# Merged attention heads stored in DRAM as one fp32 word and split where they are loaded, with a fourth probability buffer, in a hybrid encoder block

## The chip, the cores and the metric

The kernel runs on one core of a Trainium2 chip. The metric is the device time of one execution in microseconds (us). Several executions were timed; the profile is of one more execution with the hardware profiler on. MB below means 1024 KB.

## The reference

One layer of an encoder over 1024 tokens plus 16 meta tokens, width 1024, in fp32. Attention and a linear recurrence run side by side from one projection, are merged by gates, projected and followed by a SwiGLU block:

```python
xn = rmsnorm(h, norm1_g[l])
q, k, v, xr, gr, g_merge = jnp.split(xn @ w_in[l], splits, axis=-1)
attn = bidirectional_gqa(rope(q), rope(k), v)      # 8 query heads, 2 kv heads, head size 128
rnn = (rg_lru(xc, ..., False) + rg_lru(xc, ..., True)) * jax.nn.gelu(gr)
mix = g_attn * attn + g_rnn * rnn                  # gates are sigmoids of g_merge
h = h + mix @ w_out[l]
hn = rmsnorm(h, norm2_g[l])
g, u = jnp.split(hn @ w_ffn_in[l], 2, axis=-1)
h = h + (jax.nn.silu(g) * u) @ w_ffn_out[l]
```

The change touches `mix`, on its way from the attention to the product with `w_out`.

## The kernel before, in words

PE multiplies in a form of fp32 that it rounds. So every operand is kept as two halves, a rounded high part and the rest: `split` (line 95) copies the value to the high part on ACT (L96) and subtracts that from the value on DVE or POOL (L97); `mm3` (line 99) makes each product from three matmuls. A head's merged output thus takes twice the space of its fp32 value when it is stored split.

The stage in question is the attention, about 500 to 830 us of the span. It walks over 8 heads `h` and, in each, 8 tiles `i` of 128 queries, so over 64 tiles. `emit_scores` (line 572) does one tile: nine score matmuls into one of two PSUM tiles `S0`, `S1`, row maximum on DVE (L585), exponential on ACT (L588), then the probabilities in two fp16 halves into a buffer `PP` (L594 and L595 on ACT, L597 on DVE) and one transposing DMA (L600) from `PP` to `PT`. There are three `PP` buffers, taken in turn, so a tile writes the one that the transpose of three tiles earlier has read. Every second tile, `emit_pv` (line 604) multiplies the 256 transposed probabilities of two tiles (a *unit* `u`, four in a head) with V in 25 matmuls (L611). That is done two units behind: the product of a unit stands on PE after the scores of the second unit that follows.

Behind the product, `emit_pv` merges: DVE multiplies by the gate (L613), POOL adds the recurrent branch (L614), and the result of 256 columns is split into `mst` (ACT L96, POOL L97) and stored with both halves to `mix_d` in DRAM (L618, on SP's queue). Only the first half of head 7 is split straight into the operand `M` in SBUF (L621).

Between the tiles PE has other work: the gate projection of a later head (`ga_steps`, six matmuls behind a tile, `gap`), and in head 7 the output projection of the first four heads (`out_half`, tile `oph`). For the projection, `load_mix(kh, c)` (line 645) brings four heads of one half of the columns back to SBUF, both halves of the words, with two DMAs issued by POOL (L650) straight into `M`. `load_wout` (line 654) brings a block of `w_out` through one of three `raw` buffers and splits it on ACT and POOL. The table `ahead` (line 694) says behind which tile `(h, i)` these loads are written.

All DMAs but those of `load_mix` stand in one queue, SP's: transposes, loads of Q, of the recurrent branch (`gar`), of weights and of the residual rows (`h`), and the stores. A framework's scheduler orders each engine's instructions; it moves loads ahead of where the program writes them, and a `raw` buffer must be free before SP may issue into it. SP's queue is in order: what waits there holds everything behind it.

Of the kernel before, what the change touches and what calls it, by code (L numbers as in the profile page):

```python
# [8 lines left out]
F32 = mybir.dt.float32  # L9
F32R = mybir.dt.float32r  # L10
F16 = mybir.dt.float16
# [8 lines left out]
T = 1024  # L20
# [3 lines left out]
NH = 8  # L24
# [9 lines left out]
KPAIR = KLO + T  # L34
# [8 lines left out]
def tile_hybrid_encoder_block(  # L43
# [25 lines left out]
    V, S, G, PE, SP = nc.vector, nc.scalar, nc.gpsimd, nc.tensor, nc.sync  # L69

    x = x[0]
    out = out[0]
# [5 lines left out]
    dram = ctx.enter_context(tc.tile_pool(name="dram", bufs=1, space=bass.MemoryType.DRAM))  # L78
# [7 lines left out]
    def page(shape, dtype, name):  # L86
        return pages.tile(shape, dtype, tag="pg", name=name)

    def raw_tile(shape):
        return rawp.tile(shape, F32, tag="raw", name="raw")  # L90

    def f32(ap):
        return ap.bitcast(F32)

    def split(src, hi, lo, eng=None):
        S.activation(out=hi, in_=src, func=AF.Copy)  # L96
        (eng or V).tensor_tensor(out=lo, in0=src, in1=f32(hi), op=ALU.subtract)  # L97

    def mm3(ps, terms):
        n = len(terms)  # L100
        for k, (lh, ll, rh, rl) in enumerate(terms):
            PE.matmul(out=ps, lhsT=lh, rhs=rh, start=(k == 0), stop=False)  # L102
            PE.matmul(out=ps, lhsT=lh, rhs=rl, start=False, stop=False)  # L103
            PE.matmul(out=ps, lhsT=ll, rhs=rh, start=False, stop=(k == n - 1))  # L104
# [10 lines left out]

    q_d = [dram.tile([HD, T], F32, name=f"q_d{h}") for h in range(NH)]
    rm_d = [dram.tile([128, T], F32, name=f"rm_d{b}") for b in range(NB)]
    mix_d = [dram.tile([2, 4, 128, T], F32, name=f"mix_d{kh}") for kh in range(2)]

    def rstd(sq_sum, n, count, tag, scale=1.0):  # L120

# [435 lines left out]
    p2 = p2_pool.__enter__()  # L557
# [3 lines left out]
    def fill_bank(name):  # L561
        return ps2.tile([128, 512], F32, tag="fill", bufs=2, name=name)

    SB = [ps2.tile([128, 3, 512], F32, name=f"S{i}") for i in range(2)]
    PP = [p2.tile([128, KPAIR], F16, bufs=1, name=f"PP{i}") for i in range(3)]
    for p in PP:
        G.memset(p[:, T:KLO], 0.0)

# [3 lines left out]
    def emit_scores(h, i, q):  # L572
        kv = h // 4
        n = n_tile[0]
        n_tile[0] += 1
        s = SB[n % 2]
        pair = PP[n % 3]
        if n < 2:
            PE.matmul(out=s[:, 2, NK - 2 * KC:KC], lhsT=ones, rhs=mask, start=True, stop=True)
        for j in range(3):  # L580
            a, e = KC * j, min(KC * j + KC, NK)
            qs = slice(128 * i, 128 * i + 128)
            mm3(s[:, j, 0:e - a], [(q[:, 0, qs], q[:, 1, qs], kT[:, 0, kv, a:e], kT[:, 1, kv, a:e])])
        nm = small.tile([128, 1], F32, name="nm")
        V.tensor_reduce(out=nm, in_=s[:, :, 0:KC], axis=AX.XY, op=ALU.max, negate=True)  # L585
        p = p2.tile([128, 3, KC], F32, name="p")
        den = small.tile([128, 1], F32, name="den")
        S.activation(out=p, in_=s[:, :, 0:KC], func=AF.Exp, bias=nm, accum_out=den)  # L588
        r = small.tile([128, 1], F32, name="pr")
        V.tensor_scalar(out=den, in0=den, scalar1=2.0 ** -14, scalar2=None, op0=ALU.mult)  # L590
        V.reciprocal(out=r, in_=den)
        pf = p.rearrange("p j k -> p (j k)")[:, 0:NK]

        S.activation(out=pair[:, 0:NK], in_=pf, func=AF.Copy, scale=r)  # L594
        S.activation(out=pair[:, T + 64:T + 64 + NM], in_=pf[:, T:NK], func=AF.Copy, scale=r)  # L595
        for a, e, o in ((0, T, KLO), (T, NK, T + 32)):
            V.scalar_tensor_tensor(out=pair[:, o:o + e - a], in0=pf[:, a:e], scalar=r, in1=pair[:, a:e], op0=ALU.mult, op1=ALU.subtract)  # L597
        if i % 2 == 0:
            PT[h, i // 2] = p2.tile([128, 17, 256], F16, name="PT")
        SP.dma_start_transpose(  # L600
            out=PT[h, i // 2][:, :, 128 * (i % 2):128 * (i % 2) + 128], in_=pair,
        )

    def emit_pv(h, u, gar):
        kv = h // 4
        pt = PT.pop((h, u))
        ps = fill_bank("pv")[:, 0:256]
        vs = slice(HD * kv, HD * kv + HD)
        terms = [(j, 0, j) for j in range(9)] + [(j, 0, 9 + j) for j in range(8)] + [(j, 1, j) for j in range(8)]
        for n, (j, hl, m) in enumerate(terms):  # L610
            PE.matmul(out=ps, lhsT=vt[:, j, hl, vs], rhs=pt[:, m], start=(n == 0), stop=(n == len(terms) - 1))  # L611
        c = slice(256 * u, 256 * u + 256)
        V.tensor_tensor(out=gar[:, 0, c], in0=gar[:, 0, c], in1=ps, op=ALU.mult)  # L613
        G.tensor_tensor(out=gar[:, 1, c], in0=gar[:, 0, c], in1=gar[:, 1, c], op=ALU.add)  # L614
        if h < NH - 1 or u >= 2:
            st = p2.tile([128, 2, 256], F32R, name="mst")
            split(gar[:, 1, c], st[:, 0], st[:, 1], G)
            SP.dma_start(out=mix_d[h // 4][:, h % 4, :, c].rearrange("l d t -> d l t"), in_=f32(st))  # L618
        elif u % 2 == 1:
            cs = slice(256 * u - 256, 256 * u + 256)  # L620
            split(gar[:, 1, cs], M[0][1][0][:, 3], M[1][1][0][:, 3])  # L621

    def load_gar(h):
        g = page([128, 2, T], F32, "gar")
        SP.dma_start(out=g[:, 1], in_=rm_d[h])
        return g
# [15 lines left out]

    M = [[[None, None], [None, None]], [[None, None], [None, None]]]

    def load_mix(kh, c):

        k = 3 if kh and not c else 4
        for hl in range(2):
            M[hl][kh][c] = page([128, 4, 512], F32R, f"M{hl}{kh}{c}")
            G.dma_start(out=M[hl][kh][c][:, 0:k], in_=mix_d[kh][hl, 0:k, :, 512 * c:512 * c + 512].rearrange("h d t -> d h t"))  # L650

    wo = {}

# [31 lines left out]
    def out_steps():  # L685
# [5 lines left out]
    gar = {0: ga0, 1: load_gar(1)}  # L691
    steps = ga_steps(w_ga, gar[1])

    ahead = {
        (6, 4): [(load_mix, 0, 0)],
        (6, 6): [(load_wout, 0, 0), (load_wout, 1, 0)],
        (6, 7): [(load_h, 0, page, [0])],
        (7, 2): [(load_h, 0, page, [1])],
        (7, 3): [(load_wout, 0, 1)],
        (7, 4): [(load_mix, 1, 0)],  # L700
        (7, 5): [(load_wout, 1, 1)],
        (7, 6): [(load_wout, 2, 0)],
        (7, 7): [(load_wout, 3, 0), (load_wout, 2, 1), (load_wout, 3, 1)],
    }
    for h in range(NH):
        for i in range(8):
            emit_scores(h, i, q)
            if i == 1 and h + 1 < NH:
                q_n = load_head(h + 1)
            if i == 3 and h + 2 < NH:  # L710
                w_ga = load_block(COL_GA + 128 * (h + 2), G)
                gar[h + 2] = load_gar(h + 2)
            for fn, *a in ahead.get((h, i), ()):
                fn(*a)
            if i == 5 and h + 2 < NH:
                steps = ga_steps(w_ga, gar[h + 2])
            if (h, i) == (NH - 1, 0):
                steps = out_steps()
            if i % 2 == 1:
                if len(pend) > 1:  # L720
                    u = pend.pop(0)
                    emit_pv(*u, gar[u[0]])
                pend.append((h, i // 2))
            for _ in range(2 if h == 0 and i < 3 else 1):
                next(steps, None)
        q = q_n
    for _ in steps:
        pass
    load_mix(0, 1)
    for k in range(4):  # L730
        if k % 2 == 0 and pend:
            u = pend.pop(0)
            emit_pv(*u, gar[u[0]])
        for _ in out_half(k, 0, 1, SB[k // 3][:, k % 3]):
            pass
# [337 lines left out]
    for n, (i, j) in enumerate(chunks):  # L1073
        if n + AHEAD < len(chunks):
            c = chunks[n + AHEAD]
# [96 lines left out]
```

## Time and profile before

| what | value |
|---|---|
| three timed runs | 1540.11, 1540.17 (median), 1542.09 us |
| the profiled execution | 1543.0 us, of it 1541.2 us from the first to the last instruction |
| PE busy | 1484.2 us, 96% |
| DVE busy | 1101.1 us, 71% |
| ACT busy | 743.1 us, 48% |
| POOL busy | 325.3 us, 21% |
| HBM | 137.15 MB read, 56.36 MB written |

A busy PE is a matmul in flight. Since PE is busy nearly everywhere, the places to look for are the few stretches where it is not, and those where its granted clock is below full speed. The DMA share is the mean busy share of the 16 DMA engines, and goes above 1 where packets of several queues overlap.

### The profile page before, as it was taken

How to read it: one execution, taken by the hardware profiler on the slowest of the kernel's cores; microseconds unless marked ns; L12 is line 12 of the kernel's file. 1: busy time of each engine (PE TensorE's matmuls, PEld its weight loads, DVE VectorE, ACT ScalarE, POOL GpSimd, SP SyncE). 2: the span in 40 equal slices, each digit the busy share in tenths (PEclk: the TensorE clock that was granted, in tenths of full speed). 3: DMA queues.
4: the chain of work that ended last, by engine and by line, in shares of the span. 5: the costliest groups of instructions: out<-in, count | busy, mean ns of one | idle time of the engine just before them, and what ended most of it. 6: DMA issues, size and time to landing. Idle time of an engine off the chain costs nothing. (4 is left out here: it accounts for less than half of the span.)

```text
span 1541.2 us, 20211 instructions
## 1 busy us (share of the span) xinstructions
PE 1484.2 (96%) x7323; PEld 1241.6 (81%) x7323; DVE 1101.1 (71%) x1712; ACT 743.1 (48%) x1264; POOL 325.3 (21%) x243
## 2 busy tenths in 40 slices
PE   6999999999999899997889979999999999999999
PEld 4888888888888788886778857888888888788887
DVE  6888677777776777786764697777777777667562
ACT  5544476677667666666651352322222222364330
POOL 0000000000000544444341253333333333300000
PEclk9999999999999999999999989999999999999999
DMA  6123311122212799999997215444444444699641
GB/s 240 41 77 101 88 33 60 60 62 62 63 55 78 167 201 201 202 199 228 234 228 246 69 40 165 164 157 158 157 157 158 157 158 157 230 378 330 205 149 66
DMA packets 310196, 230.49 MB, mean 150 GB/s; under 512 B 151016, under 2 KB 252352, under 8 KB 310096
## 3 DMA queue, kind: packets, MB, share of 16 engines
q1 hardware_dynamic: 306128, 221.34, 50.9%
q0 software_dynamic: 3968, 7.86, 1.9%
q8 instruction: 57, 0.93, 0.2%
q14 instruction: 43, 0.35, 0.1%
HBM read 137.15 MB, written 56.36 MB: 126 GB/s over the span
## 5 line engine op out<-in xcount | busy, mean ns | idle before, releaser
L96 ACT ACTIVATE wS<-s 128x512 fp32r<-128x512 f32 x88 | 53.2, 628 | 169.2 <-DVE s L880 51.6
L597 DVE SCALAR_TENSOR_TENSOR PP<-p,pr,PP 128x1024 f16<-128x1024 f32 (+1 forms) x128 | 119.4, 986 | 20.2 <-ACT PP L594 20.0
L96 ACT ACTIVATE pw<-pr 128x1024 fp32r<-128x1024 f32 x77 | 81.0, 1061 | 104.8 <-PE po L1088 63.4
L1086 PE MATMUL po<-pw 128*128 128x512 f32 x308 | 120.4, 391 | 1.5 <-ACT pw L96 1.5
L1087 PE MATMUL po<-pw 128*128 128x512 f32 x308 | 120.6, 391 | 0.8 <-DVE pw L97 0.8
L1088 PE MATMUL po<-pw 128*128 128x512 f32 x308 | 120.3, 391 | 0.0
L97 DVE TENSOR_TENSOR pw<-pr,pw 128x1024 fp32r<-128x1024 f32 x77 | 94.0, 1251 | 36.1 <-ACT pw L96 29.7
L611 PE MATMUL pv<-PT,vt 128*128 128x256 f16 x800 | 97.7, 281 | 17.6 <-DMA PT<-PP 16.9
L588 ACT ACTIVATE p<-S,nm 128x1044 f32<-128x1044 f32 x64 | 72.2, 1129 | 68.2 <-DVE nm L585 65.7
L611 PEld LDWEIGHTS <-vt 128*128 128x128 f16 x800 | 78.0, 101 | 33.5 <-issue 18.3
L97 DVE TENSOR_TENSOR wS<-s,wS 128x512 fp32r<-128x512 f32 x88 | 70.5, 818 | 16.9 <-ACT wS L96 16.0
L594 ACT ACTIVATE PP<-p,pr 128x1040 f16<-128x1040 f32 x64 | 73.9, 1155 | 15.2 <-DMA PT<-PP 10.3
L585 DVE TENSOR_REDUCE nm<-S 128x1 f32<-128x1044 f32 x64 | 76.8, 1231 | 2.1 <-PE S L104 2.1
L433 POOL MEMSET xrp<- 128x2 f32 x8 | 0.9, 108 | 349.8 <-DVE xc L440 349.8
L102 PE MATMUL S<-kT,qh 128*128 128x348 f32 (+1 forms) x192 | 63.6, 331 | 6.7 <-ACT p L588 6.4
L1086 PEld LDWEIGHTS po<-pw 128*128 128x128 f32 x308 | 58.1, 189 | 14.1 <-ACT pw L96 1.9
L1087 PEld LDWEIGHTS po<-pw 128*128 128x128 f32 x308 | 58.2, 189 | 13.0 <-DVE pw L97 1.1
L1088 PEld LDWEIGHTS po<-pw 128*128 128x128 f32 x308 | 58.2, 189 | 12.2
L103 PE MATMUL S<-kT,qh 128*128 128x348 f32 (+1 forms) x192 | 62.1, 323 | 0.0
L104 PE MATMUL S<-kT,qh 128*128 128x348 f32 (+1 forms) x192 | 62.0, 323 | 0.0
L97 DVE TENSOR_TENSOR wA<-raw,wA 128x512 fp32r<-128x512 f32 x60 | 50.3, 842 | 15.9 <-ACT wA L96 15.9
L103 PE MATMUL xr<-xn,wblk 128*128 128x264 f32 (+1 forms) x192 | 61.4, 320 | 0.0
(308 smaller groups left out, 4467.0 us busy)
## 6 DMA issues: line engine op xcount, KB each, us to landing
raw<-in_w_ffn_in_dram SPq DMA_DIRECT2D x47, 512.0 KB, 4.8
raw<-in_w_in_dram SPq DMA_DIRECT2D x44, 512.0 KB, 4.1
pr<-act_d SPq DMA_DIRECT2D x77, 256.0 KB, 5.3
raw<-in_w_ffn_out_dram SPq DMA_DIRECT2D x22, 512.0 KB, 4.6
wot_d<-bs SPq DMA_DIRECT2D x44, 256.0 KB, 4.5
act_d<-as SPq DMA_DIRECT2D x44, 256.0 KB, 2.0
pr<-wot_d SPq DMA_DIRECT2D x44, 256.0 KB, 5.3
act_d<-act SPq DMA_DIRECT2D x33, 256.0 KB, 3.3
```

The source lines that it names most:

```text
L96: S.activation(out=hi, in_=src, func=AF.Copy)
L97: (eng or V).tensor_tensor(out=lo, in0=src, in1=f32(hi), op=ALU.subtract)
L102: PE.matmul(out=ps, lhsT=lh, rhs=rh, start=(k == 0), stop=False)
L103: PE.matmul(out=ps, lhsT=lh, rhs=rl, start=False, stop=False)
L585: V.tensor_reduce(out=nm, in_=s[:, :, 0:KC], axis=AX.XY, op=ALU.max, negate=True)
L588: S.activation(out=p, in_=s[:, :, 0:KC], func=AF.Exp, bias=nm, accum_out=den)
L594: S.activation(out=pair[:, 0:NK], in_=pf, func=AF.Copy, scale=r)
L597: V.scalar_tensor_tensor(out=pair[:, o:o + e - a], in0=pf[:, a:e], scalar=r, in1=pair[:, a:e], op0=ALU.mult, op1=ALU.subtract)
L611: PE.matmul(out=ps, lhsT=vt[:, j, hl, vs], rhs=pt[:, m], start=(n == 0), stop=(n == len(terms) - 1))
L1086: PE.matmul(out=banks[t], lhsT=lh, rhs=w[:, 0, 1], start=j == 0, stop=False)
L1087: PE.matmul(out=banks[t], lhsT=lh, rhs=w[:, 1, 1], start=False, stop=False)
L1088: PE.matmul(out=banks[t], lhsT=ll, rhs=w[:, 0, 1], start=False, stop=j == NFP - 1)
```

## The change

It has three parts. The merged head is stored as its fp32 word, 512 columns at a time, from the `gar` tile itself: `mst` and its split are gone. `load_mix` loads the words of two heads at a time through a `raw` buffer, on SP's queue, and splits them there into `M` (ACT and POOL for the first half of the columns, ACT and DVE for the second). A fourth `PP` buffer is added.

```diff
--- before.py
+++ after.py
@@ -115,7 +115,7 @@
 
     q_d = [dram.tile([HD, T], F32, name=f"q_d{h}") for h in range(NH)]
     rm_d = [dram.tile([128, T], F32, name=f"rm_d{b}") for b in range(NB)]
-    mix_d = [dram.tile([2, 4, 128, T], F32, name=f"mix_d{kh}") for kh in range(2)]
+    mix_d = [dram.tile([4, 128, T], F32, name=f"mix_d{kh}") for kh in range(2)]
 
     def rstd(sq_sum, n, count, tag, scale=1.0):
 
@@ -562,7 +562,7 @@
         return ps2.tile([128, 512], F32, tag="fill", bufs=2, name=name)
 
     SB = [ps2.tile([128, 3, 512], F32, name=f"S{i}") for i in range(2)]
-    PP = [p2.tile([128, KPAIR], F16, bufs=1, name=f"PP{i}") for i in range(3)]
+    PP = [p2.tile([128, KPAIR], F16, bufs=1, name=f"PP{i}") for i in range(4)]
     for p in PP:
         G.memset(p[:, T:KLO], 0.0)
 
@@ -574,7 +574,7 @@
         n = n_tile[0]
         n_tile[0] += 1
         s = SB[n % 2]
-        pair = PP[n % 3]
+        pair = PP[n % 4]
         if n < 2:
             PE.matmul(out=s[:, 2, NK - 2 * KC:KC], lhsT=ones, rhs=mask, start=True, stop=True)
         for j in range(3):
@@ -612,12 +612,12 @@
         c = slice(256 * u, 256 * u + 256)
         V.tensor_tensor(out=gar[:, 0, c], in0=gar[:, 0, c], in1=ps, op=ALU.mult)
         G.tensor_tensor(out=gar[:, 1, c], in0=gar[:, 0, c], in1=gar[:, 1, c], op=ALU.add)
-        if h < NH - 1 or u >= 2:
-            st = p2.tile([128, 2, 256], F32R, name="mst")
-            split(gar[:, 1, c], st[:, 0], st[:, 1], G)
-            SP.dma_start(out=mix_d[h // 4][:, h % 4, :, c].rearrange("l d t -> d l t"), in_=f32(st))
-        elif u % 2 == 1:
-            cs = slice(256 * u - 256, 256 * u + 256)
+        if u % 2 == 0:
+            return
+        cs = slice(256 * u - 256, 256 * u + 256)
+        if h < NH - 1 or u == 3:
+            SP.dma_start(out=mix_d[h // 4][h % 4, :, cs], in_=gar[:, 1, cs])
+        else:
             split(gar[:, 1, cs], M[0][1][0][:, 3], M[1][1][0][:, 3])
 
     def load_gar(h):
@@ -642,12 +642,15 @@
 
     M = [[[None, None], [None, None]], [[None, None], [None, None]]]
 
-    def load_mix(kh, c):
-
-        k = 3 if kh and not c else 4
+    def load_mix(kh, c, eng=None):
+
         for hl in range(2):
             M[hl][kh][c] = page([128, 4, 512], F32R, f"M{hl}{kh}{c}")
-            G.dma_start(out=M[hl][kh][c][:, 0:k], in_=mix_d[kh][hl, 0:k, :, 512 * c:512 * c + 512].rearrange("h d t -> d h t"))
+        for k in range(0, 4, 2):
+            n = 1 if kh and not c and k else 2
+            raw = raw_tile([128, 2, 512])[:, 0:n]
+            SP.dma_start(out=raw, in_=mix_d[kh][k:k + n, :, 512 * c:512 * c + 512].rearrange("h d t -> d h t"))
+            split(raw, M[0][kh][c][:, k:k + n], M[1][kh][c][:, k:k + n], eng)
 
     wo = {}
 
@@ -692,12 +695,12 @@
     steps = ga_steps(w_ga, gar[1])
 
     ahead = {
-        (6, 4): [(load_mix, 0, 0)],
+        (6, 4): [(load_mix, 0, 0, G)],
         (6, 6): [(load_wout, 0, 0), (load_wout, 1, 0)],
         (6, 7): [(load_h, 0, page, [0])],
         (7, 2): [(load_h, 0, page, [1])],
         (7, 3): [(load_wout, 0, 1)],
-        (7, 4): [(load_mix, 1, 0)],
+        (7, 4): [(load_mix, 1, 0, G)],
         (7, 5): [(load_wout, 1, 1)],
         (7, 6): [(load_wout, 2, 0)],
         (7, 7): [(load_wout, 3, 0), (load_wout, 2, 1), (load_wout, 3, 1)],
```

The scheduler places the new instructions. In the rows below, `PP_4500` to `PP_4502` are the three probability buffers (`PP_4503` the fourth), `M_...` a tile of merged heads, and `mix_d_92` and `mix_d_93` the merged heads 0 to 3 and 4 to 7 in DRAM.

SP's queue before, around tiles 4 to 8 of head 5 (the first two transposes shown are those of its tiles 4 and 5):

```order
L625 DMA gar<-rm_d_91 128x1024
L618 DMA mix_d_93<-mst 128x2x256
L656 DMA raw<-in_w_out_dram 128x2x512
L600 DMA_TRANSPOSE PT<-PP_4502 128x17x128
L600 DMA_TRANSPOSE PT<-PP_4500 128x17x128
L618 DMA mix_d_93<-mst 128x2x256
L600 DMA_TRANSPOSE PT<-PP_4501 128x17x128
L600 DMA_TRANSPOSE PT<-PP_4502 128x17x128
L618 DMA mix_d_93<-mst 128x2x256
L668 DMA h<-in_x_dram 128x1024 x2
L656 DMA raw<-in_w_out_dram 128x2x512
L600 DMA_TRANSPOSE PT<-PP_4500 128x17x128
```

The same place in the changed kernel; the first two transposes shown are again those of tiles 4 and 5:

```order
L625 DMA gar<-rm_d_91 128x1024
L659 DMA raw<-in_w_out_dram 128x2x512
L600 DMA_TRANSPOSE PT<-PP_4500 128x17x128
L600 DMA_TRANSPOSE PT<-PP_4501 128x17x128
L659 DMA raw<-in_w_out_dram 128x2x512 x2
L619 DMA mix_d_93<-gar 128x512
L600 DMA_TRANSPOSE PT<-PP_4502 128x17x128
L600 DMA_TRANSPOSE PT<-PP_4503 128x17x128
L671 DMA h<-in_x_dram 128x1024 x2
L652 DMA raw<-mix_d_93 128x2x512
L600 DMA_TRANSPOSE PT<-PP_4500 128x17x128
```

Two loads of `w_out` now stand together behind the first pair, one store in place of two, and half of the load of heads 4 to 7 stands behind the residual rows. Loads of heads 0 to 3 stood on POOL's queue before and are on SP's by now, behind the transposes of tiles 3 and 5 of head 4.

POOL before, at the load of heads 4 to 6:

```order
L614 TENSOR_TENSOR gar<-gar 128x256
L650 DMA M_7287<-mix_d_93 128x3x512
L97 TENSOR_TENSOR mst<-gar,mst 128x256
L650 DMA M_7289<-mix_d_93 128x3x512
L97 TENSOR_TENSOR wo<-raw,wo 128x2x512
```

What stands in its place on SP in the changed kernel, between tiles 5 and 6 of head 6:

```order
L600 DMA_TRANSPOSE PT<-PP_4501 128x17x128
L619 DMA mix_d_93<-gar 128x512
L652 DMA raw<-mix_d_93 128x512
L659 DMA raw<-in_w_out_dram 128x2x512
L600 DMA_TRANSPOSE PT<-PP_4502 128x17x128
```

The store of head 6, its load and a load of `w_out` stand in front of the transpose of tile 6; the load reads what the store writes, and so waits for its landing.

SP before, around tiles 2 to 5 of head 7 (`PP_4501` first is tile 2):

```order
L618 DMA mix_d_93<-mst 128x2x256
L656 DMA raw<-in_w_out_dram 128x2x512
L600 DMA_TRANSPOSE PT<-PP_4501 128x17x128
L618 DMA mix_d_93<-mst 128x2x256
L656 DMA raw<-in_w_out_dram 128x2x512
L600 DMA_TRANSPOSE PT<-PP_4502 128x17x128
L859 DMA raw<-in_w_ffn_in_dram 128x8x128 x2
L600 DMA_TRANSPOSE PT<-PP_4500 128x17x128
L600 DMA_TRANSPOSE PT<-PP_4501 128x17x128
L859 DMA raw<-in_w_ffn_in_dram 128x8x128
```

And in the changed kernel (`PP_4502` is tile 2):

```order
L659 DMA raw<-in_w_out_dram 128x2x512
L619 DMA mix_d_93<-gar 128x512
L659 DMA raw<-in_w_out_dram 128x2x512 x2
L600 DMA_TRANSPOSE PT<-PP_4502 128x17x128
L600 DMA_TRANSPOSE PT<-PP_4503 128x17x128
L652 DMA raw<-mix_d_92 128x2x512 x2
L600 DMA_TRANSPOSE PT<-PP_4500 128x17x128
L600 DMA_TRANSPOSE PT<-PP_4501 128x17x128
L652 DMA raw<-mix_d_93 128x2x512
```

Three loads of `w_out` now stand in front of tile 2, and loads of merged heads take the place of those of `w_ffn_in`, which stand behind the stage. PE's rows keep their order but for seven matmuls of the projection into `S`, which stand 36 matmuls earlier behind the last scores. Nothing else moves on PE.

## Rows read from the trace of the kernel before

**Rows 1.** Busy by stretch: PE, PEld, DVE, ACT, POOL; PE clock, DMA share, GB/s.

```profile
540.00:700.00 160.00, 155.48 (x1006) 135.75 (x1005) 126.17 (x201) 106.77 (x180) 74.51 (x55) 1.00 1.00 199
700.00:800.00 100.00, 83.10 (x518) 71.31 (x516) 74.53 (x113) 62.22 (x100) 46.11 (x34) 0.93 1.12 240
800.00:890.00 90.00, 90.00 (x448) 74.69 (x447) 47.62 (x94) 22.13 (x44) 19.64 (x19) 1.00 0.50 152
```

**Rows 2.** PE in order of time: start us, us, idle before it.

```profile
518.41 0.66 PE L102 MATMUL S<-kT,qh 128*128 128x348 f32 x1 [3.64 <-ACT p L588]
...
708.12 2.90 PE L611 MATMUL pv<-PT,vt 128*128 128x256 f16 x25
...
724.41 4.97 PE L611 MATMUL pv<-PT,vt 128*128 128x256 f16 x25 [7.78 <-DMA PT<-PP]
...
743.23 2.90 PE L611 MATMUL pv<-PT,vt 128*128 128x256 f16 x25
...
750.53 2.90 PE L611 MATMUL pv<-PT,vt 128*128 128x256 f16 x25 [1.54 <-DMA PT<-PP]
...
760.74 2.89 PE L611 MATMUL pv<-PT,vt 128*128 128x256 f16 x25 [2.74 <-DMA PT<-PP]
...
769.11 2.90 PE L611 MATMUL pv<-PT,vt 128*128 128x256 f16 x25
...
781.33 5.49 PE L611 MATMUL pv<-PT,vt 128*128 128x256 f16 x25 [3.69 <-DMA PT<-PP]
...
792.30 2.90 PE L611 MATMUL pv<-PT,vt 128*128 128x256 f16 x25
```

**Rows 3.** DMA issues, 707 to 766 us: count, KB each, us to landing.

```profile
M<-mix_d POOLq DMA_DIRECT2D x2, 1024.0 KB, 10.8
h<-in_x_dram SPq DMA_DIRECT2D x4, 512.0 KB, 5.4
mix_d<-mst SPq DMA_DIRECT2D x6, 256.0 KB, 4.0
raw<-in_w_out_dram SPq DMA_DIRECT2D x3, 512.0 KB, 6.8
PT<-PP SPq DMA_TRANSPOSE x12, 5.7
```

**Rows 4.** SP in order of time: two pairs of transposes, start us, us.

```profile
697.96 5.01 SPq L600 DMA_TRANSPOSE PT<-PP  x2
...
707.42 12.26 SPq L600 DMA_TRANSPOSE PT<-PP  x2
```

**Rows 5.** By line, 510 to 830 us: count, busy us, mean ns, idle.

```profile
L97 POOL TENSOR_TENSOR mst<-gar,mst 128x256 fp32r<-128x256 f32 x30 | 39.6, 1319 | 34.4 <-ACT mst L96 34.4
...
L97 POOL TENSOR_TENSOR wo<-raw,wo 128x1024 fp32r<-128x1024 f32 x8 | 18.9, 2358 | 14.7 <-ACT wo L96 14.7
...
L96 ACT ACTIVATE mst<-gar 128x256 fp32r<-128x256 f32 x30 | 12.3, 409 | 29.9 <-POOL gar L614 29.9
...
L96 ACT ACTIVATE wo<-raw 128x1024 fp32r<-128x1024 f32 x8 | 8.4, 1047 | 2.6 <-DMA raw<-in_w_out_dram 2.6
```

**Rows 6.** Waits, 540 to 700 us: total us, times, longest us.

```profile
PE S L102 <- ACT p L588: 2.5, 5, 0.8
...
ACT PP L594 <- DMA PT<-PP: 1.0, 1, 1.0
```

**Rows 7.** Waits, 700 to 830 us: total us, times, longest us.

```profile
ACT PP L594 <- DMA PT<-PP: 9.0, 5, 4.8
```

**Rows 8.** The store of merged heads (tile mst), issue to landing.

```profile
DMA to landing us min/median/max: 2.7/3.7/6.5
```

**Rows 9.** Behind the stage: fourth row norm on DVE, first use on PE.

```profile
841.18 1.28 DVE L138 SCALAR_TENSOR_TENSOR y<-h,nr,g2b 128x1024 f32<-128x1024 f32 x1
...
849.82 1.03 PE L787 MATMUL hT<-ident,y 128*128 128x128 f32 x8
```

## The prediction

> **What bounds the kernel now.** I read the busy time by stretch first. From 540 to 700 us PE is busy for 155.48 of 160 us at full clock, and from 800 to 890 us all the time; from 700 to 800 us it is busy for 83.10 of 100 at a mean clock of 0.93, while the DMA share rises from 1.00 to 1.12 and the rate from 199 to 240 GB/s [rows 1]. So the change can win little before 700 us and nothing behind 800; the stretch between is where to look. No other engine is full in it: DVE has 74.53, ACT 62.22 us.
>
> Next, PE in order of time, to see what it waits for. The starts of the products with V show the pace: 8.37 us from one to the next where nothing is missing (760.74 to 769.11), and 5.76 (7.30 less a wait of 1.54, from 743.23 to 750.53) at the end of head 6, where no filler stands between the tiles [rows 2]. Five units lie between the starts at 708.12 and 760.74, of 52.62 us; at pace they take 4 x 8.37 + 5.76 = 39.2, so **13.4 us** are lost. From 769.11 to 792.30 two units take 23.19 in place of 16.7: **6.5 us** lost. All four waits there, the longest 7.78 us, end with the DMA PT<-PP, the transposed probabilities; and the products behind the two longest run at 4.97 and 5.49 us in place of 2.90, which is in the loss.
>
> Then the DMA issues, to see why the transposes are late. Two transposes issued alone take 5.01 us; the pair at 707.42 takes 12.26 [rows 4]. Beside it POOL issues two loads of 1 MB each into M, which take 10.8 us to land [rows 3]. **The DMA engines are the bound of this stretch, and the merged heads are a large part of their load.**
>
> From this a price. The 59 us from 707 to 766 carry 12 transposes, 30.1 us at half of 5.01 each, and 2 x 1 + 4 x 0.5 + 6 x 0.25 + 3 x 0.5 = 7.0 MB of other transfers [rows 3]. The other 28.9 us make 4.1 us per MB. The pair at 707.42 gives another: 7.25 us more for 2 MB, 3.6 per MB.
>
> **The change, part by part.**
>
> *Bytes, first stretch.* Counted from the order on SP, for the same 12 transposes (tile 4 of head 5 to tile 7 of head 6): three loads of w_out (1.5 MB), four of residual rows (2.0), three stores of merged heads (0.75), and 0.5 + 0.25 of the load of heads 4 to 6: 5.0 MB in place of 7.0. Heads 0 to 3 have been loaded by then, in head 4, where PE is the bound. 2.0 MB at 4.1 are 8.2 us. The transfers would still need 30.1 + 20.5 = 50.6 us, against 5 x 8.37 + 5.76 = 47.6 of PE for the six units, so DMA remains the longer and the whole 8.2 counts.
>
> *Bytes, second stretch*, the eight transposes of head 7: before, 1.5 MB into M, two stores, two loads of w_out and three of w_ffn_in, 4.5 MB; now three loads of w_out, one store and three of merged heads, 3.75 MB. 0.75 MB at 4.1 are 3.1 us. Here too DMA remains longer: 20.0 + 15.4 = 35.4 us against 4 x 8.37 = 33.5. Together 11.3 us, or 9.9 at 3.6 per MB.
>
> The 240 GB/s of the row [rows 1] is the rate that the engines sustain among transposes. The Trainium skill (DMA: Bandwidth & Descriptors, Specifications) gives about 358 GB/s as the limit of HBM per core; an estimate by it is 2.9 us per MB, and the two terms would be 8.1 us in place of 11.3. The sum goes by the row.
>
> *Work on the engines.* Gone are 30 splits of mst, 12.3 us on ACT and 39.6 on POOL. Added are eight splits of a load: at the 1.047 and 2.358 us of a w_out block, some 8 us on ACT and 9 on POOL, the other four subtractions on DVE [rows 5]. Between 540 and 700 us nothing takes the place of mst, but PE waits there for ACT only 2.5 us in five waits [rows 6]. I take 1 us of it, between 0 and 2.5.
>
> *The fourth buffer.* ACT waited for a buffer 1.0 us from 540 to 700 us, and 9.0 from 700 to 830, all behind late transposes [rows 6, 7]. A buffer more lets ACT run ahead one tile; it does not make a transpose earlier when the engines are behind. I take 0, between 0 and what is left of the late waits.
>
> *Loads moved to SP.* Each issue costs SP about what a store did, and eight loads come for fifteen stores that go: nothing. But SP is in order. The load of head 6 waits for the store just ahead of it, 3.7 us to land [rows 8], where before POOL waited; tiles 6 and 7 of head 6 are queued behind, then their product. Also, two loads of w_out behind the pair of tiles 4 and 5 of head 5 wait for POOL's splits of M to free their raw buffers. Their cover is the time in which the next pair's probabilities are made; if it is gone, up to 3.7 us come back. I take 0, since DMA has work queued while SP waits and PE is paced by all of it together.
>
> *Behind the stage.* The last load of heads 4 to 7 now waits for a store that goes out without mst in between, then is split on ACT and DVE, and stands in front of the first row norms there. The fourth row norm ends at 842.5 and the first transpose of normed rows is at 849.82 [rows 9], 7.3 us of room. A store's 3.7 and two DVE splits of about as long as a row norm (1.28) are 6.3: covered. If not, 1 to 3 us.
>
> *The start of the stage.* PE's 3.64 us at 518.41 wait for the first exponentials [rows 2], not for a buffer: nothing.
>
> **Sum.** 8.2 + 3.1 + 1.0 = 12.3 us off 1543.0, the profiled execution's own time: 1530.7. The runs' median, 1540.17, lies 2.8 below that execution, so I forecast **1528**.
>
> **The rivals.**
>
> *All the waits go.* The price of a MB may hold only for the burst on POOL's queue; spread out, the transfers may fit under PE's pace. For it: from 540 to 700 us PE keeps its pace with DMA at a share of 1.00. Against it: the tally above still comes out above PE's need. Then 13.4 + 6.5 + 1 to 2 are won: 1519, and 1515 if the wait at the start goes too.
>
> *The loads bunch.* In front of three pairs in a row stand 1.25, 1.5 and 1.25 MB, 5.1, 6.2 and 5.1 us at 4.1, where a pair leaves 8.37 - 5.01 = 3.4 free: 6.2 us late instead of the tally's 3.0. In front of tile 2 of head 7 stand 1.75 MB, 3.8 late instead of 1.9; and the wait of the load for its store adds 3.7. That is 8.8 less won than forecast, some 3.5 us in all: 1537. With half of it, 1532. For it: waits of 1.54 and 2.74 us came on pairs that by SP's order had 1.25 MB in front [rows 2].
>
> *No change.* The transposes' own chain, scores to PT, is what is late, and the loads are hidden: within 3 us of before. Against it: the long waits begin with the M loads; before them PE lost 4.5 us in 160 [rows 1].
>
> *SP's queue holds the transposes.* What decides is one mechanism: eight loads, each in front of a pair, that hold SP for what they wait on (a store, or POOL freeing a raw buffer). At 3.7 us each, the landing of a store, that is 29.6 us against 12.3 won: 17 slower, 1557. It turns the sign from 1.5 us per load. For it: PT is what PE waits for, so there is little lead. Against it: one load of eight within the stage has its store right in front; most raw buffers are freed tiles before. By the Trainium skill (DMA: Bandwidth & Descriptors, Queues, rings and completion order) descriptors of one queue are consumed in ring order on each engine, while different queues take turns; by that rule a load on SP goes wholly ahead of the transposes, where one on POOL's queue shared with them. The pair of 12.26 us beside POOL's loads shows that sharing was no protection either.
>
> **How the numbers follow.** The forecast, with 8 to 16 us won: 0.45. All waits go: 0.2. Bunching, 3 to 8 us won: 0.17. No change: 0.08. Slower: 0.1. About 0.2%, 3.1 us, is what a measurement of this kernel can tell from no change. Faster is then 0.45 + 0.2 + 0.17 = 0.82, the same 0.08, slower 0.1. The range leaves out the slower case and most of no change: from 1514, with the wait at the start gone, to 1538, where bunching has eaten nearly all.
>
> **What would show it.** Right: no M load on POOL; the wait of 7.78 us and the slow products gone; waits on PT left, each under 3 us, in heads 6 and 7; from 540 to 700 us little changed; the product starts from tile 4 of head 5 to the end of head 6 closer by about 8 us; the residual adds and row norms as before. Wrong: SP's transposes waiting on POOL or on a store's landing with PE idle behind them; PE waiting on ACT or DVE between 700 and 800 us; or PE idle between 825 and 860 us.

## The result, and the profile after

The changed kernel takes **1525.28 us** (median of four runs, 1522.90 to 1526.96), the kernel before beside it 1540.95 (four runs, 1540.11 to 1542.09). The ratio is **0.9892**, 95% interval 0.9876 to 0.9907: 15.7 us less. The forecast was 1528, with a range of 1514 to 1538. The profiled execution took 1524.24 us, 1522.4 of it from the first to the last instruction, against 1541.2 before: 18.8 us less by the profiles.

Busy by stretch after, the columns those of [rows 1]:

```profile
540.00:700.00 160.00, 160.00 (x1050) 142.37 (x1049) 124.12 (x210) 107.07 (x171) 52.07 (x38) 1.00 0.99 196
700.00:800.00 100.00, 90.76 (x556) 77.90 (x555) 70.02 (x114) 58.69 (x89) 39.60 (x24) 0.97 0.99 213
800.00:890.00 90.00, 82.75 (x402) 68.45 (x401) 59.80 (x108) 31.54 (x59) 23.29 (x17) 1.00 0.33 112
```

From 540 to 700 us PE is now busy all the time, where it lost 4.5 us. From 700 to 800 it is busy for 90.76 us at a clock of 0.97, in place of 83.10 at 0.93, and the rate fell from 240 to 213 GB/s. The last row shows no new loss: two waits on the second norm, 1.75 and 5.45 us, which ended behind 890 us, now end at 877.5 and 889.6 and take 1.76 and 5.48.

PE in order of time after, answering to [rows 2]:

```profile
701.52 2.90 PE L611 MATMUL pv<-PT,vt 128*128 128x256 f16 x25
...
714.66 0.50 PE L636 MATMUL gap<-xn,wblk 128*128 128x512 f32 x1 [1.88 <-ACT gar L543]
721.97 2.90 PE L611 MATMUL pv<-PT,vt 128*128 128x256 f16 x25
730.34 2.90 PE L611 MATMUL pv<-PT,vt 128*128 128x256 f16 x25
735.94 0.66 PE L102 MATMUL S<-kT,qh 128*128 128x348 f32 x1 [2.70 <-ACT p L588]
740.37 2.90 PE L611 MATMUL pv<-PT,vt 128*128 128x256 f16 x25
747.74 2.90 PE L611 MATMUL pv<-PT,vt 128*128 128x256 f16 x25
757.42 2.90 PE L611 MATMUL pv<-PT,vt 128*128 128x256 f16 x25 [1.14 <-DMA PT<-PP]
...
778.40 2.89 PE L611 MATMUL pv<-PT,vt 128*128 128x256 f16 x25 [0.88 <-DVE h L685]
```

The unit that started at 708.12 before starts at 701.52, the one at 760.74 at 747.74, the ones at 769.11 and 792.30 at 757.42 and 778.40. The 7.78 us are gone, every product runs at 2.9 us, and one wait of 1.14 us on PT is left. In their place stand waits on ACT, 1.88 and 2.70 us, that were not there before, and behind both the granted clock falls for a while: its mean is 0.79 from 712 to 720 and again from 732 to 740 us, with 1.00 between 724 and 732.

DMA issues after, 707 to 766 us, answering to [rows 3]:

```profile
raw<-in_w_out_dram SPq DMA_DIRECT2D x6, 512.0 KB, 5.2
h<-in_x_dram SPq DMA_DIRECT2D x4, 512.0 KB, 4.9
mix_d<-gar SPq DMA_DIRECT2D x4, 256.0 KB, 4.7
raw<-mix_d SPq DMA_DIRECT2D x1, 512.0 KB, 6.6
raw<-mix_d SPq DMA_DIRECT2D x1, 256.0 KB, 3.1
PT<-PP SPq DMA_TRANSPOSE x12, 4.6
```

No load of M stands on POOL, and a transpose lands 4.6 us after its issue, in place of 5.7. The window is the one of [rows 3] in time; the changed kernel is 13 us ahead at its end, so that transfers of later tiles fall into it. Counted by tile, from the transposes of tile 4 of head 5 (699.37) to those of tile 7 of head 6 (748.59), SP issued just the 5.0 MB of the prediction's tally.

The splits that took mst's place, 510 to 830 us, answering to [rows 5], and the longest of ACT's waits from 700 to 830 us (total us, times, longest us), where [rows 7] had ACT wait for a buffer:

```profile
L96 ACT ACTIVATE M<-raw 128x1024 fp32r<-128x1024 f32 x7 | 7.3, 1054 | 33.9 <-DMA mix_d<-gar 17.4 <-PE oph L681 10.4 <-DMA raw<-mix_d 4.8
L97 POOL TENSOR_TENSOR M<-raw,M 128x1024 fp32r<-128x1024 f32 x3 | 7.1, 2373 | 9.2 <-ACT M L96 9.2
...
ACT M L96 <- DMA mix_d<-gar: 17.4, 2, 11.3
```

The longer of the two waits in 17.4, 11.3 us, stands at the end of the stage, and PE does not wait behind it. The first is in ACT's order of time, with the exponential for which PE waits at 735.94 queued behind it:

```profile
733.24 1.06 ACT L96 ACTIVATE M<-raw 128x1024 fp32r<-128x1024 f32 x1 [6.01 <-DMA mix_d<-gar]
734.20 0.58 ACT L543 ACTIVATE gar<-gap 128x512 f32<-128x512 f32 x1
734.68 1.12 ACT L588 ACTIVATE p<-S,nm 128x1044 f32<-128x1044 f32 x1
```

Its load was issued at 716.70 and takes 6.6 us, so it is not what was late. By the order of the instructions this copy also waits for the landing of head 5's two stores: the high half of M takes the page that head 5's `gar` had, and the stores now read `gar` itself. Before, mst stood between, and the page came free with its last split.

**Where the time went.** Three marks make a ledger for all kernels: the first product with V, the 21st, and the first transpose of a normed row. In the kernel before, with the third mark, 849.82, in [rows 9]:

```profile
525.26 2.90 PE L611 MATMUL pv<-PT,vt 128*128 128x256 f16 x25
...
699.76 2.90 PE L611 MATMUL pv<-PT,vt 128*128 128x256 f16 x25
```

In the changed one:

```profile
525.52 2.90 PE L611 MATMUL pv<-PT,vt 128*128 128x256 f16 x25
...
693.17 2.90 PE L611 MATMUL pv<-PT,vt 128*128 128x256 f16 x25
...
834.87 1.04 PE L790 MATMUL hT<-ident,y 128*128 128x128 f32 x8
```

| stretch | before | after | won |
|---|---|---|---|
| first to 21st product | 174.5 | 167.7 | 6.8 |
| 21st product to first row transpose | 150.1 | 141.7 | 8.4 |
| from there to the end | 691.4 | 687.5 | 3.9 |

The last line is no gain of the change: in the twelve other kernels below that stretch takes 686.3 to 688.4 us, in those that store and load the heads as before too. The profiled execution of before was 3 to 4 us long there, which is also why it lay 2.8 above its median. So the two stretches of the stage won 15.2 us, close to the 15.7 of the medians: 6.8 where 1.0 was forecast, and 8.4 where 11.3 were.

### The profile page after: what moved, and what is told of

Read it like the earlier page. It is cut to its first block, busy times and chain, and to the rows that moved or that the text cites. A ratio compares the mean times of both kernels' runs of the same rounds, so it can differ in the third digit from the quotient of the medians.

```text
span 1522.4 us, 20097 instructions
## 1 busy us (share of the span) xinstructions
PE 1478.0 (97%) x7323; PEld 1240.4 (81%) x7323; DVE 1091.5 (72%) x1716; ACT 740.3 (49%) x1242; POOL 289.0 (19%) x210
## 5 line engine op out<-in xcount | busy, mean ns | idle before, releaser
L597 DVE SCALAR_TENSOR_TENSOR PP<-p,pr,PP 128x1024 f16<-128x1024 f32 (+1 forms) x128 | 103.5, 867 | 11.6 <-ACT PP L594 11.4
L611 PE MATMUL pv<-PT,vt 128*128 128x256 f16 x800 | 93.0, 273 | 2.0 <-DMA PT<-PP 1.1
```

## The experiments

All of them, with the median and the ratio to the kernel before that ran beside them (1539.8 to 1541.0 us), and the two stretches of the ledger in the profiled execution. That lies within 2 us of its kernel's median, but for three: 2 us below in the run of bytes and queue alone, 3 above with POOL's subtractions and 4 above with rows before weights.

| kernel | us | ratio, 95% interval | to 21st product | to row transpose |
|---|---|---|---|---|
| changed | 1525.28 | 0.9892 [0.9876, 0.9907] | 167.7 | 141.7 |
| before + four buffers (in place) | 1544.19 | 1.0019 [1.0003, 1.0035] | 173.3 | 155.2 |
| before, in place, three buffers | 1544.48 | 1.0023 [1.0011, 1.0034] | 173.6 | 155.1 |
| before, half the bytes | 1537.42 | 0.9983 [0.9974, 0.9992] | 173.4 | 148.1 |
| changed, three buffers | 1530.12 | 0.9933 [0.9918, 0.9949] | 168.4 | 147.4 |
| changed, mst's work back | 1533.14 | 0.9954 [0.9938, 0.9969] | 174.4 | 145.7 |
| changed, bytes back | 1534.87 | 0.9961 [0.9947, 0.9974] | 167.7 | 152.6 |
| changed, loads on POOL's queue | 1531.15 | 0.9938 [0.9926, 0.9951] | 168.3 | 147.3 |
| changed, other page for M | 1527.33 | 0.9912 [0.9899, 0.9926] | 167.8 | 144.5 |
| changed, three buffers and mst's work | 1537.11 | 0.9971 [0.9960, 0.9982] | 174.0 | 145.5 |
| changed, ACT's copies back | 1525.75 | 0.9902 [0.9888, 0.9916] | 167.7 | 142.7 |
| changed, POOL's subtractions back | 1533.70 | 0.9955 [0.9942, 0.9969] | 174.9 | 146.7 |
| changed, rows before weights | 1524.78 | 0.9905 [0.9888, 0.9921] | 167.6 | 145.1 |

### The fourth buffer

```diff
-    PP = [... for i in range(3)]
+    PP = [... for i in range(4)]
-            st = p2.tile([128, 2, 256], F32R, name="mst")
+            st = gar[:, :, c].bitcast(F32R)
```

There is no room for it beside mst, so the head is split in place.

> The kernel before with a fourth probability buffer and nothing else of the change. Room for it is made by splitting a merged head in place in the gar tile, both halves stored as before, so the bytes, the split work and the queues are those of before. Theory (bytes): the late transposes of 700 to 800 us stay, so 1537 to 1541 us; of the 4.5 us that PE lost from 540 to 700 us at most what hung on a buffer comes back. Rival (buffer): if ACT's running one tile further ahead is what emptied the waits, PE is busy for 160 of 160 us from 540 to 700 and also closer to full from 700 to 800, for 1530 us or less.

Measured: 1544.19 us, a little slower than before and above the theory's 1537 to 1541. The buffer did what it is for: the profile names no wait of ACT for one between 700 and 800 us (9.0 us in [rows 7]; two idle stretches of ACT before the same operation, 6.5 us together, it puts down to nothing), and PE gained nothing by it. What it lost came from the other line of the edit, which the same kernel with three buffers shows:

> The kernel before with three buffers as it was, and a merged head split in place in the gar tile, both halves stored from there: what the run with four buffers alone had beside its buffer. A gar page is then free only when its last store has landed, in place of when its last split is done. Theory (that page, not the buffer, is what made the run with four buffers slower than before): 1541 to 1546 us. Rival (the fourth buffer itself costs there): 1539 to 1541 us, as before.

Measured: 1544.48 us. ACT's waits from 700 to 800 us in it:

```profile
ACT PP L594 <- DMA PT<-PP: 8.8, 5, 2.8
ACT wo L96 <- DMA mix_d<-gar: 6.7, 1, 6.7
ACT qh L96 <- DMA mix_d<-gar: 3.2, 1, 3.2
```

The last two are pages of `gar` held until a store lands, as in the changed kernel. Added to the kernel before with its heads split in place, **the buffer is worth nothing** (1544.19 against 1544.48, a difference well inside their intervals). Taken from the changed kernel it costs 5 us:

> The changed kernel with three probability buffers in place of four. Theory (bytes): 1525 to 1527 us, with PE still busy for nearly all of 540 to 700 us. Rival (buffer): the waits of ACT for a buffer come back, PE is at about 155.5 of 160 us from 540 to 700, and late transposes cost more from 700 to 800: 1530 us or more.

Measured: 1530.12 us; by the ledger 0.8 us are lost up to the 21st product, 5.7 behind. The rival's 155.5 of 160 was wrong, PE keeps 159.37, but its time was right. So the buffer counts in the changed kernel and not in the one before. How it counts is not shown: the rival's waits did not come back either, ACT waits for a buffer just once between 700 and 800 us, for 0.8 us.

What differs earlier is DVE beside POOL, the subject of the run on the split work below: its low halves of two tiles take 5.44 and 5.41 us, from 700.05 and from 711.11, beside POOL's sums and its subtractions for M and then for `w_out`, where the changed kernel has one such round, of 5.46 from 706.19, beside a sum and those for `w_out`. Whether the missing buffer is what moved them together, no run tells.

### The bytes

In the kernel before, half of them taken away:

```diff
-            SP.dma_start(out=mix_d[...][:, h % 4, :, c]..., in_=f32(st))
+            SP.dma_start(out=mix_d[...][0, h % 4, :, c], in_=f32(st)[:, 0])
-            G.dma_start(out=M[hl]..., in_=mix_d[kh][hl, ...])
+            if hl == 0:
+                G.dma_start(out=M[hl]..., in_=mix_d[kh][hl, ...])
...
-                lh, ll = (M[hl][kh][c]... for hl in range(2))
+                lh = ll = M[0][kh][c]...
```

> The kernel before with only the high half of each merged head stored and loaded; the low half is still made but neither stored nor loaded, and the projection multiplies the high half in its place, so the low half is left out of the result. Bytes fall as in the change, while mst's work, its 30 stores, POOL's queue for the loads and three buffers stay. Theory (bytes): the waits on the transposes between 708 and 800 us shrink by 10 to 15 us, 1526 to 1531 us, and 540 to 700 us stays near 155.5 of 160. Rival (buffer, queue or the split work made the gain): 1537 us or more.

Measured: 1537.42 us, 2.4 less than before, near the rival's 1537 and far from the theory's 1526 to 1531. Half the bytes alone win 2.0 us behind the 21st product; PE's four waits on PT from 700 to 800 us are still 10.8 us, of the 15.8 of the kernel before:

```profile
PE pv L611 <- DMA PT<-PP: 10.8, 4, 4.3
```

In the changed kernel, the bytes put back:

```diff
             SP.dma_start(out=mix_d[h // 4][h % 4, :, cs], in_=gar[:, 1, cs])
+            SP.dma_start(out=mx2_d[h // 4][h % 4, :, cs], in_=gar[:, 1, cs])
...
             SP.dma_start(out=raw, in_=mix_d[kh]...)
+            SP.dma_start(out=f32(M[1][kh][c])[:, k:k + n], in_=mx2_d[kh]...)
```

> The changed kernel with each of its 15 stores made a second time into a spare place in DRAM, and beside each load of merged heads a second load of the same size into the low half, which the split then overwrites. So the bytes are those of before and all else is the change's, save that the additional transfers stand on SP's queue. Prediction's theory (bytes made the gain): the waits on transposed probabilities come back between 700 and 800 us, 1535 us or more. Rival, after the first four runs (the split work and the buffer made most of it, the bytes 2 or 3 us): 1526 to 1529 us, with PE still busy for 159 or more of 160 us from 540 to 700.

Measured: 1534.87 us, at the theory's bound. Up to the 21st product nothing changes, behind it 10.9 us are lost, and PE's order of time shows by what, the late transposes and the slow products of [rows 2] again:

```profile
711.50 2.89 PE L612 MATMUL pv<-PT,vt 128*128 128x256 f16 x25 [1.16 <-DMA PT<-PP]
...
732.68 5.49 PE L612 MATMUL pv<-PT,vt 128*128 128x256 f16 x25 [3.60 <-DMA PT<-PP]
742.83 2.90 PE L612 MATMUL pv<-PT,vt 128*128 128x256 f16 x25 [1.57 <-DMA PT<-PP]
753.07 5.49 PE L612 MATMUL pv<-PT,vt 128*128 128x256 f16 x25 [3.09 <-DMA PT<-PP]
...
785.15 4.40 PE L612 MATMUL pv<-PT,vt 128*128 128x256 f16 x25 [1.96 <-DMA PT<-PP]
```

So the bytes, with the issues that carry them, are what makes the transposes late again, and 10.9 us is close to the 11.3 that the prediction priced them at. Bytes and issues this run does not tell apart, nor what hangs on POOL, whose subtractions for M wait 19.2 us in four waits for the second loads. And the run with half the bytes says that in the kernel before, most of that price was not to be won by the bytes alone.

### The split work

```diff
+        if h < NH - 1 or u >= 2:
+            st = gar[:, 0, c].bitcast(F32R)
+            split(gar[:, 1, c], st, st, G)
```

> The changed kernel with the 30 splits of merged heads done again on ACT and POOL, in place in the gar tile, for nothing; the bytes, stores and buffers are those of the change. Theory (the split work is worth the 4.5 us between 540 and 700 us): PE falls back to about 155.5 of 160 there, 1529 to 1531 us. Rival (it is worth about the 1 us of the prediction, or nothing): 1525 to 1527 us, with 159 or more of 160.

Measured: 1533.14 us, and PE at 155.28 of 160 from 540 to 700 us: the theory's mechanism, and more than its 4.5 us (its time was 1529 to 1531). All but 0.1 us of what was won up to the 21st product is lost again (174.4 us against 174.5 before), and 4.0 us behind it.

Which half of the split? The copy on ACT alone, then the subtraction on POOL alone:

```diff
+            S.activation(out=gar[:, 0, c], in_=gar[:, 1, c], func=AF.Copy)
```

> The changed kernel with the 30 copies of merged heads done again on ACT, without the subtractions on POOL. Theory (what cost PE 540 to 700 us was POOL's subtraction beside DVE: DVE's products of 128x16 took 570 ns there with it and take 350 without it): PE is busy for 159 or more of 160 us, those products stay near 350 ns, 1525 to 1528 us. Rival (the copies, which stand in ACT's order between the exponentials and wait for POOL's sum): PE at about 155.5 of 160, 1530 us or more.

```diff
+            G.tensor_tensor(out=gar[:, 0, c].bitcast(F32R), in0=gar[:, 1, c], in1=gar[:, 0, c], op=ALU.subtract)
```

> The changed kernel with 30 subtractions of 128x256 on POOL behind its sums, without the copies on ACT. Theory (POOL beside DVE): PE loses time again between 540 and 700 us, 157 of 160 or less, with DVE's products of 128x16 well above 350 ns, 1529 us or more. Rival (ACT's copies): PE at 159 or more of 160, 1525 to 1527 us.

Measured: 1525.75 us with the copies, no change; 1533.70 with the subtractions, all of it. Busy by stretch from 540 to 700 us, the copies first, then the subtractions:

```profile
540.00:700.00 160.00, 160.00 (x1051) 142.44 (x1051) 124.08 (x212) 114.70 (x192) 51.99 (x38) 1.00 1.00 196
```

```profile
540.00:700.00 160.00, 154.92 (x1001) 135.42 (x1000) 126.77 (x201) 100.40 (x163) 79.04 (x53) 1.00 0.95 186
```

How POOL, an engine with half its time free, holds up PE, is in DVE's rows. The operation that makes the low half of the probabilities of the 16 meta tokens, by form, from 540 to 700 us (count, busy us, mean ns), before, after, with the copies and with the subtractions:

```profile
L597 DVE SCALAR_TENSOR_TENSOR PP<-p,pr,PP 128x16 f16<-128x16 f32 x37 | 21.1, 570 | 0.0
```

```profile
L597 DVE SCALAR_TENSOR_TENSOR PP<-p,pr,PP 128x16 f16<-128x16 f32 x38 | 13.3, 350 | 0.0
```

```profile
L597 DVE SCALAR_TENSOR_TENSOR PP<-p,pr,PP 128x16 f16<-128x16 f32 x39 | 13.5, 347 | 0.0
```

```profile
L597 DVE SCALAR_TENSOR_TENSOR PP<-p,pr,PP 128x16 f16<-128x16 f32 x37 | 21.8, 589 | 0.0
```

And in order of time, before, DVE's rows and then POOL's: the low halves of two tiles (x4) beside a subtraction on POOL.

```profile
634.79 3.81 DVE L597 SCALAR_TENSOR_TENSOR PP<-p,pr,PP 128x1024 f16<-128x1024 f32 x4 [0.36 <-ACT PP L594]
...
644.22 3.80 DVE L597 SCALAR_TENSOR_TENSOR PP<-p,pr,PP 128x1024 f16<-128x1024 f32 x4 [0.38 <-ACT PP L594]
...
652.72 3.51 DVE L597 SCALAR_TENSOR_TENSOR PP<-p,pr,PP 128x1024 f16<-128x1024 f32 x4 [0.36 <-ACT PP L594]
656.16 2.38 DVE L585 TENSOR_REDUCE nm<-S 128x1 f32<-128x1044 f32 x2
...
670.03 3.81 DVE L597 SCALAR_TENSOR_TENSOR PP<-p,pr,PP 128x1024 f16<-128x1024 f32 x4 [0.36 <-ACT PP L594]
...
654.53 1.68 POOL L97 TENSOR_TENSOR mst<-gar,mst 128x256 fp32r<-128x256 f32 x1 [1.33 <-ACT mst L96]
```

DVE after; beside the row of 647.28 stands only a sum of 0.74 us on POOL:

```profile
630.27 3.33 DVE L597 SCALAR_TENSOR_TENSOR PP<-p,pr,PP 128x1024 f16<-128x1024 f32 x4 [0.33 <-ACT PP L594]
...
647.28 3.03 DVE L597 SCALAR_TENSOR_TENSOR PP<-p,pr,PP 128x1024 f16<-128x1024 f32 x4 [0.36 <-ACT PP L594]
...
663.79 3.32 DVE L597 SCALAR_TENSOR_TENSOR PP<-p,pr,PP 128x1024 f16<-128x1024 f32 x4 [0.33 <-ACT PP L594]
```

The four take half a microsecond longer beside POOL, and the row maxima stand right behind them on DVE. The exponentials wait for the maxima, PE's next scores for the exponentials. A round of that loop goes from the four of a pair of tiles to the next four. Rounds differ by what else falls into them, so take the four of a head: 35.24 us before (634.79 to 670.03) and 33.52 after (630.27 to 663.79), where PE needs 4 x 8.37 = 33.5. Before, the loop through DVE is slower than PE; after, PE sets the pace. DVE's waits from 540 to 700 us say the same. After, its row maxima wait for PE's scores, and before they never do:

```profile
DVE nm L585 <- PE S L104: 3.1, 6, 0.6
```

The loss comes late in the stretch: the first ten products with V span 75.9 us before and 75.5 after, the 10th to the 21st 98.6 and 92.2. That PE lives on a lead until then is my reading. DVE's operations with an input in PSUM are not slowed: the product with the gate takes 410 and 411 ns before and after, the row maximum 1231 and 1237.

The Trainium skill (SBUF — State Buffer, SBUF: two separate sides) has a rule for this: DVE and GpSimd share a pair of ports, which an operation holds for its whole length, and for a DVE operation with two inputs in SBUF this counts against a GpSimd operation that reads SBUF. The rows agree in what is slowed; they show one engine beside the other, not a lock. The copies on ACT, which cost nothing, agree too.

### The queue

```diff
-            SP.dma_start(out=raw, in_=mix_d[kh]...)
+            G.dma_start(out=raw, in_=mix_d[kh]...)
```

> The changed kernel with the loads of merged heads issued by POOL in place of SP; bytes, buffers and split work are the change's. Theory (the queue matters: loads on POOL's queue bunch with the transposes): waits on transposed probabilities of 5 us or more between 700 and 800 us, 1528 us or more. Rival (the queue does not matter): 1524 to 1527 us.

Measured: 1531.15 us, the time of the theory, but not its mechanism: PE waits nowhere on PT between 700 and 800 us. It waits for ACT and DVE:

```profile
PE S L102 <- ACT p L588: 6.5, 2, 3.3
PE oph L680 <- DVE gar L613: 4.4, 2, 2.4
PE gap L636 <- ACT gar L543: 2.1, 1, 2.1
```

ACT's copies for M wait 4.8 us for a load and 5.1 for a store's landing (the page) there, with the exponentials queued behind them. That the loads, now behind POOL's own work, come later is what I take from it; it was not shown by a run of its own.

### Bytes and queue alone

The changed kernel with three buffers and the splits of the run with mst's work.

> The changed kernel with three probability buffers and with the splits of merged heads done again for nothing: what is left of the change are the bytes and SP's queue. Theory (the parts add up: 8 us for the split work, 5 for the buffer, 2 to 3 for bytes and queue): 1536 to 1540 us. Rival (bytes and queue together are worth more than the high halves alone were, 2.4 us): 1529 to 1534 us.

Measured: 1537.11 us, 3.4 less than before. Here the parts add up about as the theory said. One by one they don't: taken from the changed kernel, the buffer costs 6.5 us in the two stretches, the split work 10.7, the bytes 10.9, the queue 6.2, together 34 where 15.2 were won. By the medians it is 4.8, 7.9, 9.6 and 5.9, together 28 where 15.7 were.

### The two new waits

The load of heads 4 to 6 written one step later, so that M takes another page:

```diff
-        (7, 4): [(load_mix, 1, 0, G)],
-        (7, 5): [(load_wout, 1, 1)],
+        (7, 5): [(load_wout, 1, 1), (load_mix, 1, 0, G)],
```

> The changed kernel with the load of heads 4 to 6 written one step later, behind the load of a w_out block, so that the high half of its operand takes another page: by the order of the instructions its copy on ACT then waits for its load alone and no longer for the landing of the stores of head 5, whose gar page it took. Theory (that wait of 6.0 us on ACT, with the exponentials queued behind it, is what makes PE wait 2.70 us and run slowly around 736 us): the wait is gone and 2 to 4 us are won, 1521 to 1523 us. Rival (something else is late at that place by then): 1524 to 1527 us.

Measured: 1527.33 us, the rival's time and not the theory's 1521 to 1523. The wait of ACT for the page is gone, as expected, and PE's 2.70 us are 1.84, but nothing is won: PE now waits 5.2 us on PT from 700 to 800 us, which it did for 1.1. Then both waits at once, with a page and with POOL's subtractions for w_out apart:

```diff
-        (6, 6): [(load_wout, 0, 0), (load_wout, 1, 0)],
-        (6, 7): [(load_h, 0, page, [0])],
+        (6, 6): [(load_h, 0, page, [0]), (load_wout, 0, 0)],
+        (6, 7): [(load_wout, 1, 0)],
```

> The changed kernel with the first residual rows loaded before the two first blocks of w_out, and those two blocks one tile apart. By the order of the instructions the high half of the operand of heads 4 to 6 then takes a page that no store holds, and POOL's two subtractions for w_out no longer stand back to back. Theory (the two new waits, 1.88 us behind those subtractions at 714 us and 2.70 us behind the page at 736 us, each with a slow clock behind it, are worth 2 to 5 us): 1520 to 1523 us. Rival (the loads, which stand closer together, take it back, as in the run with another page): 1525 to 1528 us.

Measured: 1524.78 us, the same as the changed kernel within its interval, and short of the theory's 1520 to 1523. PE's waits from 700 to 800 us in its profiled execution, which took 4 us more than the median, so that they may be longer than most:

```profile
PE S L102 <- ACT p L588: 9.3, 6, 3.6
PE pv L611 <- DMA PT<-PP: 4.2, 2, 2.6
```

The named waits are gone (none on `gar`, none of ACT on a store), and others of the same size stand elsewhere. No version beat the changed kernel by more than can be measured, and what bounds the rest of this stretch stays open. In the changed kernel the eight units from 701.52 to 778.40 take 76.9 us, 12.5 more than seven at 8.37 and one at 5.76.

## Why the prediction was right, and where it was not

The time, 1528 for 1525.28, and its sign came out, and so did the main mechanism, transposes that come earlier with fewer bytes. That the sum came so close is luck in part: two errors offset each other, 2.9 us too many behind the 21st product and 5.8 too few ahead of it. Also, the base was an execution whose end, untouched by the change, took 3.9 us more than after; the 2.8 us taken off for it happened to make up for most of that.

*Bytes, first stretch (8.2).* Five units, from the 708.12 of [rows 2] on, took 52.62 us and now take 46.22: **6.4 us**, by all parts of the change together. The tally counted on DMA being the longer. PE's waits in it are now on ACT, and there, as I read it, the last 2 us went. The first of them, 1.88 us, stands behind a DVE round in which the low halves of two tiles took 5.46 us beside POOL's sum and its subtractions for `w_out`: POOL's splits slow the same loop there.

*Bytes, second stretch (3.1).* 23.19 us became 20.98: 2.2. Between the two stretches 1.3 are lost, from the last on to the first row transpose 1.0 won.

The price of the bytes, 4.1 us per MB, agrees with the run that puts them back: 10.9 us behind the 21st product, for terms of 11.3. The step that failed is the silent one, that terms may be added: half the bytes alone won 2.0 us there. My reading is that DMA, the split work and the buffer were late together in this stretch, and that the prediction looked at the one that came last; the split work was not taken out of the kernel before by itself, which would have tested it.

*Work on the engines (1.0, between 0 and 2.5).* **This term was mis-sized: put back, the split work costs 6.7 us up to the 21st product, and 10.7 in the two stretches (7.9 by the medians).** The bound was taken from PE's waits on ACT [rows 6]; PE's loss of 4.5 us in the same stretch stood in [rows 1] and came nearer. The mechanism was not the one thought of either: the step looked at ACT's order, and the run with the copies alone shows that ACT counts for nothing there. It was POOL beside DVE. The prediction listed POOL's 39.6 us in mst [rows 5] and gave them no price.

*The fourth buffer (0).* Right for the kernel before, wrong in the change: 4.8 us. The prediction let it be worth at most what is left of the late waits, and one of 1.14 us is left. By what path the buffer counts stays open.

*Loads moved to SP (0).* SP's own waits were right: two waits for a store, 2.7 us together, the longest 1.9. What was missed is that the loads now end on ACT, whose copies wait for a load or a page with the exponentials behind them. The prediction listed PE waiting on ACT between 700 and 800 us among the signs of its being wrong; it came, 7.0 us where there was none, and the waits on PT that went, 15.8 us down to 1.1, were more.

*Behind the stage, and its start (0).* Right. The fourth row norm ends at 831.5 and PE's first row transpose is at 834.9. The wait on the first exponential is 3.63 us as before.

*The rivals.* The waits did not all go, and the loads did not bunch: one wait on PT is left. SP's queue held no transpose for long. "From 540 to 700 us little changed" was the sign of being right that did not come: PE won all of its 4.5 us there.

## What to carry to other kernels

Price work on a lightly used engine by whom it stands beside: a POOL operation next to the DVE operations of a loop that runs at PE's pace can slow that loop (here 39.6 us of POOL's work were worth 8 us of the kernel's time), and PE's loss in that stretch told more of it than the waits that name an engine. Where several things are late by about as much, their prices don't add: the buffer and the bytes tried alone gave 0 and 2.4 us here, and taking any one part away cost 5 to 10. So test a part by removing it from the whole as well as by adding it to the start. When a store reads a working buffer itself in place of a staging copy, look for who takes that buffer next: it is now free only when the store has landed.

## What the runs showed of the hardware

DVE's operation on 128x16, 0.22 us at its shortest, took 0.57 us in the mean with POOL's subtractions beside it and 0.35 without; the one on 128x1024 stayed at 1.36 and 1.35. POOL's sum of 128x256 took 0.74 us where it started ahead of DVE's four (647.00 after, the four at 647.28) and 1.70 where it started behind their start (644.47 before, the four at 644.22), by spans that are rough on POOL. So both engines can pay, and on DVE the small operation is hit most. And the DMA engines' share of 1.0 was no sign that they were the bound: from 540 to 700 us it is 1.00 before and 0.99 after, with PE at 155.48 and at 160.00 of 160.
